# A macaron encoder block on one core: modulation row moved into the gate/up stage, unit loads apart from their splits, an epilogue laid out by a table

## The chip, the cores and the metric

The kernel runs on one core of one Trainium2 chip. The metric is the device time of one execution in microseconds; the time before is the median of three runs. One more execution was taken with the hardware profiler, and all views shown here come from it. In the views PE is TensorE's matmul, PEld its weight load, DVE VectorE, ACT ScalarE, POOL GpSimd, SP the sync engine whose queue issues most DMAs; L200 is line 200 of the kernel. In a list of waits, "A L1 <- B L2: 11.3, 1, 11.3" reads: the instruction A of line 1 stood idle until B of line 2 was done, in total, how often, and the longest.

## What is computed

One layer of an encoder block on x of 1024 tokens by 1024 channels, in float32. A conditioning vector c gives nine rows of 1024 through one large matrix: shift, scale and gate for each of three sub-layers.

```
mod = (silu(c) @ w_ada + b_ada).reshape(b, 3, 3, 1024)
h   = rmsnorm(x, g_pre) * (1 + scale) + shift
x  += res_w * gate * rmsnorm(fn(h), g_post)
fn  = swiglu (FFN 1), mixer (attention and a linear recurrence), swiglu (FFN 2)
swiglu(h) = (silu(h @ w_g) * (h @ w_u)) @ w_down        # 1024 -> 2816 -> 1024
softplus(-lru_lambda)                                     # eight constants per partition of the recurrence
```

## The kernel before

Every float32 product is made of three products of split operands: hi*hi, hi*lo and lo*hi. So every weight that is streamed passes through a split (L142, L143): ScalarE copies the raw tile into hi, then VectorE, or for some units GpSimd, subtracts it for lo. Tiles come from pools with a fixed number of buffers for each tag: `raw` (3), `wh` and `wl` (4 each), `t4` (22 of 4 KB per partition), and in the phase's own pool `u` (3). A DMA waits until the buffer that it is to fill is free. Inside the FFN the order of TensorE, VectorE, ScalarE and GpSimd is the order of the program, and the SP queue's order is the scheduler's, which issues a load as soon as it believes its buffer to be free; the queue itself is in order.

The FFN has two stages, each of which uses a seven-product scheme of block-wise 2x2 multiplication.

The gate/up stage works through 22 blocks of 128 hidden channels, some 19 us each for those in the scheme (blocks 4 to 21 in FFN 1). `block(fb, after)` makes seven products in the order 1, 2, 6, 5, 7, 3, 4, into the PSUM banks psX, psY and psZ. Between them stand evictions: v, a copy of psX by ScalarE (L653), must be made after the vector sum of psY (L640) and a Silu have gone through VectorE and ScalarE, and before product 7 may go on in psX. A tile `pp` with tag u lives from product 5 to product 3. After each product `after(i)` mixes the weights of the next block, advances GpSimd's jobs (sums of pairs for the down stage), and after product 3 advances a generator `early` by one step. That generator loads rows, transposes them into columns, and computes the recurrence's constants: three tiny VectorE instructions, a power on GpSimd (L968), then some twenty-two tiny VectorE instructions (L969 to L984), all in one step.

The down stage streams units of 512 KB (half a pair of activation rows and half a pair of weight rows): eleven units for each of seven passes, in the order 1, 2, 6, 5, 7, 3, 4. A unit takes twelve matmuls. `Units.fetch` loads a unit into a `raw` tile (L839) and splits it at once. `take` keeps three units ahead. In passes 2, 5 and 7 every third split has its lo on GpSimd. Seven of the units of pass 4 (j from KEPT_FROM = 4) are split early, among the units of passes 7 and 3, into t4 tiles, so that pass 4 can end its four accumulators one after the other.

During the down stage of FFN 1 a queue of background generators advances by one step for each unit of the passes 1, 2 and 6: `ada_gate(0)`, which makes the gate row of FFN 1, then `ada_cols(3)` and `ada_cols(4)`, which make the mixer's shift and scale columns. Each loads eight 512 KB blocks of w_ada and adds them up on VectorE with a factor (L198, L200); the row is then spread by matmuls with ones (L289, L290), the columns by eight small matmuls (L214). A generator that needs a PSUM bank yields BANK, and in pass 2 such a step is not taken. After pass 6, `bg_flush` runs what is left.

The epilogue, in and after pass 4, takes each of eight token blocks through `put` (sum of squares on ScalarE L321, its power -1/2 on GpSimd L322 and L323, y times gate L382), `update` (x + r*y on VectorE L388, stored, and its sum of squares) and `norm` (L399). `put` fetches x into `xr`, tag u. In FFN 1 `drain` then transposes the blocks for the next sub-layer and ScalarE evacuates them (L338, L341), while the next phase's first weights are fetched and split. In FFN 2 nothing follows, and `push_last` ends the kernel with two half updates (L443).

Of the kernel before, what the change touches and what calls it, by code (L numbers as in the profile page):

```python
# [10 lines left out]
F32 = mybir.dt.float32  # L11
# [12 lines left out]
P = 128  # L24
# [3 lines left out]
SB = S // P  # L28
# [5 lines left out]
EPS = 1e-6  # L34
NEG = -1e30
HEAD_WAIT = 8
YG_DVE = ()
LATE = 6
FIRST_NEEDS = (1,) * 8
L_WAIT = 11  # L40
# [2 lines left out]
GATES = (2, 0, 2, 4)  # L43
NORM_ACT = ()
DIRECT = {0: 4, 2: 3}
KEPT_FROM = 4


@with_exitstack
def kernel(  # L50
# [7 lines left out]
    nc = tc.nc  # L58
# [18 lines left out]
    def t4(name, dtype=F32, shape=(P, 1024)):  # L77
        return pool.tile(list(shape), dtype, tag="t4", bufs=22, name=nm(name))
# [48 lines left out]
    def load_columns_b():  # L127
        rowsB = tu("rowsB", shape=(P, P))
        nc.scalar.dma_start(rowsB[0:32, :], conv_w.rearrange("o j (k p) -> (o j k) p", p=P))
        for i, v in enumerate((conv_b, lru_ba, lru_bx, lru_lambda)):  # L130
            nc.scalar.dma_start(rowsB[32 + 8 * i : 40 + 8 * i, :], v.rearrange("o (k p) -> (o k) p", p=P))
        yield
        yield
        yield BANK
        pb = trbank("pb")
        nc.tensor.transpose(pb[:, 0:64], rowsB[0:64, :], ident[0:64, 0:64])
        nc.vector.tensor_copy(colsB, pb[:, 0:64])
        yield
# [22 lines left out]
    class Weights:  # L161
# [26 lines left out]
    def ada_acc(v, alloc):  # L188
        acc = alloc("acc")
        for k in range(KB):  # L190
            if raw_home[0] == "t4":
                raw = t4("rawa")
            else:
                raw = wpool.tile([P, 1024], F32, tag="raw", bufs=3, name=nm("rawa"))
            nc.sync.dma_start(raw, w_ada[k * P : (k + 1) * P, v * D : (v + 1) * D])
            yield None
            if k == 0:
                nc.vector.tensor_scalar(acc, raw, c_act[:, 0:1], None, op0=ALU.mult)  # L198
            else:
                nc.vector.scalar_tensor_tensor(  # L200
                    acc, raw, c_act[:, k : k + 1], acc, op0=ALU.mult, op1=ALU.add
                )
        yield None
        yield acc
# [150 lines left out]
    class Epilogue:  # L355
# [4 lines left out]
            self.y, self.r, self.r2, self.xr = {}, {}, {}, {}  # L360
            self.ready = []

        def fetch(self, sb):
            if sb < SB and sb not in self.xr:
                self.xr[sb] = tu("xr")
                nc.sync.dma_start(self.xr[sb], self.xin[sb * P : (sb + 1) * P, :])

        def push(self, sb, y):
# [5 lines left out]
                self.update(sb - 1)  # L374
            self.fetch(sb + 1)

        def put(self, sb, y, eng=None):
            self.fetch(sb)
            self.y[sb] = y
            self.r[sb] = rstd_of(y, self.eps)  # L380
            eng = eng or (nc.vector if sb in YG_DVE or sb == SB - 1 else nc.gpsimd)
            eng.tensor_tensor(y, y, gtile[self.sub], op=ALU.mult)  # L382

        def update(self, sb):
# [85 lines left out]
    def ffn(sub, w_gu, w_down, hh, hl, xin, xout):  # L470
# [217 lines left out]
        def up_phase(started):  # L688

            for fb in range(started, direct):  # L690
                for i in range(2):
                    load(fb, i)
                    cut(fb, i)
            for i in range(2):
                load(direct, i)
            for fb in range(started, direct):
                for k in range(KB):
                    part(fb, 0, k)
                    sum_step()
                finish(fb, 0)  # L700

            def first_needs():
                sum_step(100)
                for i in ORDER[:4]:
                    mix(direct, i)
                    yield
                for kk in range(4):
                    differences(kk)
                    yield
                for i in ORDER[4:]:  # L710
                    mix(direct, i)
# [12 lines left out]
            load(direct + 1, 0)  # L724
            load(direct + 1, 1)
            for fb in range(direct, NF):

                def after(i):
                    mix(fb + 1, i)
                    next(jobs, None)  # L730
                    if i == 3:
                        next(early, None)
                    if fb == NF - 1 and i in ORDER[4:]:
                        units.fetch(ORDER[4:].index(i) + 1)

                ready[0] = fb
                block(fb, after)
                for i in range(2):
                    raws.pop((fb + 1, i), None)
                    load(fb + 2, i)  # L740
            ready[0] = NF
# [80 lines left out]
        class Units:  # L822


            def __init__(self):
                self.order = [(p, j) for p in STREAM for j in range(PAIRS)]

                last, self.order = self.order[-PAIRS:], self.order[:-PAIRS]
                for n, unit in enumerate(last[KEPT_FROM:]):
                    self.order.insert(len(self.order) - 2 * PAIRS + 2 + n * 2, unit)  # L830
                self.order += last[:KEPT_FROM]
                self.n, self.got = 0, {}

            def fetch(self, n):
                while self.n < min(n, len(self.order)):
                    p, j = self.order[self.n]
                    raw = wpool.tile([P, 2, 512], F32, tag="raw", bufs=3, name=nm("rawd"))
                    for o, (t, k, half) in enumerate((act_of[p], down_of[p])):
                        nc.sync.dma_start(raw[:, o], rows(t, 2 * j + k)[:, (h1, h2)[half]])  # L839
                    if p == STREAM[-1] and j >= KEPT_FROM:  # L840
                        hi, lo = t4("dh", F32R, (P, 2, 512)), t4("dl", F32R, (P, 2, 512))
                    else:
                        hi, lo = (wpool.tile([P, 2, 512], F32R, tag=t, bufs=4, name=nm("dh")) for t in ("wh", "wl"))
                    split(raw, hi, lo, nc.gpsimd if p in (2, 5, 7) and j % 3 == 2 else nc.vector)
                    self.got[p, j] = hi, lo
                    self.n += 1

            def take(self, p, j, ahead):
                self.fetch(self.order.index((p, j)) + 1 + ahead)
                return self.got.pop((p, j))  # L850

        units = Units()
# [1 line left out]
        def down_phase(make, ahead):  # L854
# [29 lines left out]
            for p in STREAM[:-1]:  # L884
                own = p in (1, 6, 7)
                dst = chain if own else [bank("pv") for _ in range(4)]
                for j in range(PAIRS):
                    ops = units.take(p, j, 3)
                    for i in range(half):
                        mm(dst[i], i, ops, j == 0 and p not in (6, 7), j == PAIRS - 1)  # L890
                    next(jobs, None)
                    bg(1, own)
                if p == 2:
                    for _ in jobs:
                        pass
                if p == 6:
                    bg_flush()
                    raw_home[0] = "raw"
                for op, sb0, sl in reads[p]:
                    for i in range(half):  # L900
                        op(sb0 + i, sl, dst[i])

            p = STREAM[-1]
            for j in range(KEPT_FROM):
                ops = units.take(p, j, 3)
                for i in range(half):
                    mm(chain[i], i, ops, False, False)
                if j == 0:
                    units.fetch(len(units.order))
                epi.put(j, yacc[j], nc.gpsimd if j % 2 else nc.vector)  # L910
                if j > 0:
                    epi.update(j - 1)
                if j > 1:
                    epi.norm(j - 2)
                if j == KEPT_FROM - 1:
                    epi.update(j)
                    epi.norm(j - 1)
                    epi.norm(j)

            last_steps = {4: ((), (), 0), 5: ((4,), (), 3), 6: ((5,), (4,), 5), 7: ((6,), (5,), KB)}  # L920
            for i in range(half):
# [36 lines left out]
    def lru_constants():  # L958
# [7 lines left out]
        v.tensor_scalar(ax, lam, -1.0, None, op0=ALU.mult)  # L966
        v.tensor_tensor(ax, ax, lam, op=ALU.min)
        nc.gpsimd.tensor_tensor(ee, base, ax, op=ALU.pow)  # L968
        v.tensor_scalar(den, ee, 2.0, None, op0=ALU.add)  # L969
        v.reciprocal(den, den)  # L970
        v.tensor_tensor(s_, ee, den, op=ALU.mult)
# [14 lines left out]

    def mixer_constants():
        yield from load_columns_b()
        lru_constants()
        yield  # L990

    def lru_phase(hh, hl, tail):
# [785 lines left out]
```

## Time and profile before

| | us |
|---|---|
| median of three runs | 2255.58 (2254.29 to 2256.24) |
| the profiled execution | 2258.05, of which the profile's span is 2256.2 |
| TensorE busy in the span | 2163.2 (96%), 9963 matmuls |
| VectorE busy | 1327.2 (59%) |
| ScalarE busy | 1016.5 (45%) |
| GpSimd busy | 786.8 (35%) |

The mean granted clock of TensorE was 0.988 of full speed. FFN 1 fills the span up to about 750 us, FFN 2 the part from about 1590 us to the end. A busy share of TensorE says that matmuls were in flight; whether they ran at the full clock is read from the granted clock beside it. Idle time of the other engines costs nothing unless TensorE waits for it.

### The profile page before, as it was taken

To read this page: it belongs to the slowest core of one execution; us is meant where nothing else is said; L and a number is where in the kernel's file an instruction comes from. 1 tells how busy PE (TensorE), PEld (TensorE's weight loads), DVE (VectorE), ACT (ScalarE), POOL (GpSimd) and SP (SyncE) were. 2 spreads that over 40 slices of the span, in tenths; PEclk is the share of its full clock that TensorE was granted. 3 is DMA by queue.
4 is the path that set the end of the run, shared out by engine and by line. 5 is a ranking of instruction groups with operands and counts; after the bars stand their busy time and mean duration, and the time that the engine had idled before them with its cause. 6 is when DMAs were issued, how large, how long until landed. Compare 5 with 4: busy or idle time off the path is not lost. (4 is left out here: it accounts for less than half of the span.)

```text
span 2256.2 us, 26782 instructions
## 1 busy us (share of the span) xinstructions
PE 2163.2 (96%) x9963; PEld 1789.3 (79%) x9963; DVE 1327.2 (59%) x1680; ACT 1016.5 (45%) x1567; POOL 786.8 (35%) x554
## 2 busy tenths in 40 slices
PE   5999999999799999999999999999999999999998
PEld 3877788887677788888888888888778788888876
DVE  6676665455655677754425665554875665544465
ACT  3543333334244688731137776535443333334443
POOL 3458785421013301100021120005648894522114
PEclk9999999999899999999999999999999999999999
DMA  9337563358666211156511111374247663337665
GB/s 297 105 135 261 205 248 122 121 196 284 230 215 212 86 50 51 58 168 205 195 60 60 43 45 54 101 230 158 94 135 277 235 221 122 114 119 233 197 223 187
DMA packets 269595, 358.37 MB, mean 159 GB/s; under 512 B 16624, under 2 KB 178584, under 8 KB 269464
## 3 DMA queue, kind: packets, MB, share of 16 engines
q1 hardware_dynamic: 256680, 310.48, 42.6%
q10 hardware_dynamic: 12784, 46.18, 5.4%
q8 instruction: 78, 1.28, 0.2%
q14 instruction: 53, 0.43, 0.1%
HBM read 265.37 MB, written 94.37 MB: 159 GB/s over the span
## 5 line engine op out<-in xcount | busy, mean ns | idle before, releaser
L142 ACT CAST dh<-rawd 128x1024 fp32r<-128x1024 f32 x154 | 161.2, 1052 | 229.8 <-DMA rawd<-downs 86.3
L621 DVE TENSOR_TENSOR wm<-raw,wm 128x512 fp32r<-128x512 f32 x152 | 160.1, 1057 | 166.9 <-ACT wm L620 157.3
L143 DVE TENSOR_TENSOR dh<-rawd,dh 128x1024 fp32r<-128x1024 f32 x122 | 158.5, 1303 | 164.9 <-ACT dh L142 159.3
L452 PE MATMUL pj<-hh,wl 128*128 128x512 f32 x576 | 227.8, 396 | 6.3 <-DVE wl L143 4.1
L451 PE MATMUL pj<-hl,wh 128*128 128x512 f32 x576 | 227.4, 395 | 5.5 <-DVE hl L333 5.5
L450 PE MATMUL pj<-hh,wh 128*128 128x512 f32 x576 | 230.1, 400 | 1.6 <-ACT wh L142 1.0
L863 PE MATMUL px<-dh,dh 128*128 128x512 f32 x592 | 184.6, 393 | 5.5 <-POOL dh L143 3.9
L863 PE MATMUL pv<-dh,dh 128*128 128x512 f32 x528 | 166.5, 397 | 1.9 <-DVE dh L143 1.8
L143 POOL TENSOR_TENSOR wl<-raw,wh 128x1024 fp32r<-128x1024 f32 x25 | 61.5, 2469 | 298.6 <-ACT wh L142 254.1
L142 ACT CAST wh<-raw 128x1024 fp32r<-128x1024 f32 (+1 forms) x86 | 86.8, 1010 | 148.2 <-DMA raw<-in_w_in_dram 41.6
L814 POOL TENSOR_TENSOR act<-act,act 128x512 f32<-128x512 f32 x54 | 84.6, 1567 | 157.4 <-DMA act<-act 119.0
L863 PE MATMUL px<-dh 128*128 128x512 f32 x352 | 138.7, 394 | 0.4 <-ACT dh L142 0.4
L322 POOL TENSOR_SCALAR rstd<-rstd 128x1 f32<-128x1 f32 x47 | 33.3, 709 | 300.1 <-ACT junk L321 298.4
L863 PEld LDWEIGHTS px<-dh,dh 128*128 128x128 f32 x592 | 111.2, 189 | 32.0 <-POOL dh L143 4.9
L452 PEld LDWEIGHTS pj<-hh,wl 128*128 128x128 f32 x576 | 109.8, 191 | 31.0 <-DVE wl L143 5.7
L451 PEld LDWEIGHTS pj<-hl,wh 128*128 128x128 f32 x576 | 109.7, 190 | 29.4 <-DVE hl L333 7.4
L143 DVE TENSOR_TENSOR wl<-raw,wh 128x1024 fp32r<-128x1024 f32 (+1 forms) x61 | 77.7, 1274 | 88.9 <-ACT wh L142 88.9
L450 PEld LDWEIGHTS pj<-hh,wh 128*128 128x128 f32 x576 | 109.8, 191 | 24.6 <-ACT wh L142 1.7
L143 POOL TENSOR_TENSOR dh<-rawd,dh 128x1024 fp32r<-128x1024 f32 x18 | 43.0, 2390 | 246.6 <-ACT dh L142 246.6
L630 PE MATMUL psX<-hh,wm 128*128 128x512 f32 x296 | 116.5, 394 | 7.3 <-ACT mixes L653 7.3
L863 PEld LDWEIGHTS pv<-dh,dh 128*128 128x128 f32 x528 | 100.6, 191 | 25.3 <-DVE dh L143 4.3
L630 PE MATMUL psX<-hs,wm 128*128 128x512 f32 x296 | 115.5, 390 | 1.5 <-ACT mixes L646 1.4
(312 smaller groups left out, 5871.9 us busy)
## 6 DMA issues: line engine op xcount, KB each, us to landing
rawa<-in_w_ada_dram SPq DMA_DIRECT2D x56, 512.0 KB, 4.9
raw<-in_ffn_w_gu_dram SPq DMA_DIRECT2D x49, 512.0 KB, 4.6
rawd<-acts SPq DMA_DIRECT2D x88, 256.0 KB, 3.6
rawd<-downs SPq DMA_DIRECT2D x88, 256.0 KB, 3.7
raw<-in_w_in_dram SPq DMA_DIRECT2D x44, 512.0 KB, 3.9
sr<-in_ffn_w_gu_dram SPq DMA_DIRECT2D x39, 512.0 KB, 6.1
act<-act SPq DMA_DIRECT2D x37, 512.0 KB, 5.2
acts<-act ACTq DMA_DIRECT2D x36, 512.0 KB, 3.9
```

The lines of the kernel that those rows point to most:

```text
L142: nc.scalar.copy(hi, raw)
L143: (eng or nc.vector).tensor_tensor(lo, raw, hi.bitcast(F32), op=ALU.subtract)
L322: nc.gpsimd.tensor_scalar(r, r, eps, None, op0=ALU.add)
L450: nc.tensor.matmul(dst, wh[:, kk, :], xhk[:, sl], start=first, stop=False)
L451: nc.tensor.matmul(dst, wh[:, kk, :], xlk[:, sl], start=False, stop=False)
L452: nc.tensor.matmul(dst, wl[:, kk, :], xhk[:, sl], start=False, stop=last)
L621: nc.vector.tensor_tensor(t[:, 1], src, t[:, 0].bitcast(F32), op=ALU.subtract)
L630: nc.tensor.matmul(dst, t[:, 0, kk, :], xh, start=first and kk == 0, stop=False, skip_group_check=True)
L814: nc.gpsimd.tensor_tensor(o, p, q, op=op)
L863: nc.tensor.matmul(dst, a_[:, 0, tk], w_[:, 1, :], start=first and n == 0, stop=last and n == 2, skip_group_check=True,)
```

## The change

Five things are changed.

1. The constants' step has a `yield` behind the GpSimd power, so it takes two blocks. A BANK mark in the generator that loads rows is a plain yield.
2. Once `early` is used up (after block 9 of FFN 1), `after(3)` of each of the blocks 10 to 21 advances the background queue by one step. The raw tiles of w_ada then have the tag u instead of t4.
3. `Units.load` issues a unit's two DMAs, `Units.fetch` does the split. In passes 1, 2 and 6 loads run two units further ahead than splits; every second raw tile of the passes 1, 2, 6 and 5 is a t4 tile. The splits of pass 7 are all on VectorE.
4. KEPT_FROM is 5: five units of pass 4 are streamed and six kept in t4 tiles. The `put`, `update` and `norm` of the first four token blocks stand in the table FIRST_HALF. In both FFNs `put` multiplies by the gate on VectorE for every block; before, it was GpSimd for most.
5. At the start of pass 7 the x rows of the blocks 0 to 3 and 7 are fetched, 3 and 7 into t4 tiles.

```diff
-KEPT_FROM = 4
+KEPT_FROM = 5
+FIRST_HALF = (((0, 1), (), ()), ((2, 3), (0,), ()), ((), (1, 2), ()), ((), (3,), (0, 1)), ((), (), (2, 3)))
...
                 raw = t4("rawa")
+            elif raw_home[0] == "u":
+                raw = tu("rawa")
...
-            eng = eng or (nc.vector if sb in YG_DVE or sb == SB - 1 else nc.gpsimd)
+            eng = nc.vector if self.sub != 1 or sb == SB - 1 else nc.gpsimd
...
                     if i == 3:
-                        next(early, None)
+                        if next(early, BANK) is BANK and sub == 0:
+                            raw_home[0] = "u"
+                            bg(1)
+                            raw_home[0] = "raw"
...
+            def load(self, n):
+                while self.loaded < min(n, len(self.order)):
+                    p, j = self.order[self.loaded]
+                    if self.loaded % 2 and p in STREAM[:4]:
+                        raw = t4("rawd", F32, (P, 2, 512))
+                    else:
+                        raw = wpool.tile([P, 2, 512], F32, tag="raw", bufs=3, name=nm("rawd"))
+                    for o, (t, k, half) in enumerate((act_of[p], down_of[p])):
+                        nc.sync.dma_start(raw[:, o], rows(t, 2 * j + k)[:, (h1, h2)[half]])
+                    self.raws[p, j] = raw
+                    self.loaded += 1
...
-                    split(raw, hi, lo, nc.gpsimd if p in (2, 5, 7) and j % 3 == 2 else nc.vector)
+                    split(raw, hi, lo, nc.gpsimd if p in (2, 5) and j % 3 == 2 else nc.vector)
...
             def take(self, p, j, ahead):
-                self.fetch(self.order.index((p, j)) + 1 + ahead)
+                n = self.order.index((p, j)) + 1
+                self.load(n + ahead + (2 if p in STREAM[:3] else 0))
+                self.fetch(n + ahead)
...
+                if p == 7:
+                    for n in range(half):
+                        epi.fetch(n, tu if n < 3 else t4)
+                    epi.fetch(SB - 1, t4)
...
-                epi.put(j, yacc[j], nc.gpsimd if j % 2 else nc.vector)
-                if j > 0:
-                    epi.update(j - 1)
-                if j > 1:
-                    epi.norm(j - 2)
-                if j == KEPT_FROM - 1:
-                    epi.update(j)
-                    epi.norm(j - 1)
-                    epi.norm(j)
+                puts, updates, norms = FIRST_HALF[j]
+                for n in puts:
+                    epi.put(n, yacc[n])
+                for n in updates:
+                    epi.update(n)
+                for n in norms:
+                    epi.norm(n)
...
         nc.gpsimd.tensor_tensor(ee, base, ax, op=ALU.pow)
+        yield
         v.tensor_scalar(den, ee, 2.0, None, op0=ALU.add)
```

More of the change, by code (lines that the diff above doesn't have):

```diff
@@ L36 @@
 HEAD_WAIT = 8
-YG_DVE = ()
 LATE = 6
@@ L133, in load_columns_b @@
         yield
-        yield BANK
+        yield
         pb = trbank("pb")
@@ L361, in __init__, with fetch @@
             self.ready = []
-        def fetch(self, sb):
+        def fetch(self, sb, alloc=tu):
             if sb < SB and sb not in self.xr:
-                self.xr[sb] = tu("xr")
+                self.xr[sb] = alloc("xr")
                 nc.sync.dma_start(self.xr[sb], self.xin[sb * P : (sb + 1) * P, :])
@@ L375, in push, with put @@
             self.fetch(sb + 1)
-        def put(self, sb, y, eng=None):
+        def put(self, sb, y):
             self.fetch(sb)
@@ L831, in __init__ @@
                 self.order += last[:KEPT_FROM]
-                self.n, self.got = 0, {}
+                self.n, self.loaded, self.got, self.raws = 0, 0, {}, {}
+            def load(self, n):
[9 more added lines that the diff above has]
+                    self.loaded += 1
             def fetch(self, n):
+                self.load(n)
                 while self.n < min(n, len(self.order)):
                     p, j = self.order[self.n]
-                    raw = wpool.tile([P, 2, 512], F32, tag="raw", bufs=3, name=nm("rawd"))
-                    for o, (t, k, half) in enumerate((act_of[p], down_of[p])):
-                        nc.sync.dma_start(raw[:, o], rows(t, 2 * j + k)[:, (h1, h2)[half]])
+                    raw = self.raws.pop((p, j))
                     if p == STREAM[-1] and j >= KEPT_FROM:
@@ L968, in lru_constants @@
         nc.gpsimd.tensor_tensor(ee, base, ax, op=ALU.pow)
+        yield
         v.tensor_scalar(den, ee, 2.0, None, op0=ALU.add)
@@ L988, in mixer_constants @@
         yield from load_columns_b()
-        lru_constants()
+        yield from lru_constants()
         yield
```

## The prediction

> **What bounds the kernel now.** I read the page's busy shares first, then TensorE's waits, then the busy time by stretch, then the order of time in each stretch that loses.
>
> ```profile
> PE 2163.2 (96%) x9963; PEld 1789.3 (79%) x9963; DVE 1327.2 (59%) x1680; ACT 1016.5 (45%) x1567; POOL 786.8 (35%) x554
> PE pc L214 <- DVE acc L200: 11.3, 1, 11.3
> ...
> PE pt L352 <- DVE yacc L399: 4.3, 2, 3.1
> ...
> PE px L863 <- POOL dh L143: 3.9, 2, 1.9
> SPq L366 <- DVE acc L200: 8.0, 1, 8.0
> ```
>
> TensorE is busy for 2163.2 of 2256.2 us and the change takes no matmul away. All that can be won is its idle time, about 93 us, and matmuls that ran at a lower granted clock. The single wait of 11.3 us is the greatest one. The next view gives, by stretch: length, busy time (and count) of PE, PEld, DVE, ACT, POOL, granted clock, DMA share, GB/s.
>
> ```profile
> 240.00:260.00 20.00, 15.41 (x59) 12.26 (x58) 16.42 (x33) 4.87 (x9) 13.70 (x11) 0.83 0.61 215
> 330.00:500.00 170.00, 170.00 (x752) 140.81 (x751) 88.37 (x102) 59.09 (x101) 74.27 (x51) 1.00 0.44 150
> 500.00:532.00 32.00, 28.70 (x115) 22.05 (x114) 27.06 (x21) 14.45 (x18) 7.58 (x5) 0.95 0.68 232
> 532.00:590.00 58.00, 57.12 (x253) 46.90 (x251) 34.95 (x33) 20.61 (x20) 4.79 (x2) 1.00 0.92 321
> 590.00:600.00 10.00, 2.27 (x18) 1.86 (x16) 7.78 (x8) 4.04 (x6) 2.34 (x1) 0.78 0.77 270
> 600.00:610.00 10.00, 6.33 (x23) 5.75 (x24) 5.05 (x6) 0.00 (x0) 0.00 (x0) 0.50 0.20 61
> 610.00:620.00 10.00, 10.00 (x41) 8.13 (x40) 1.97 (x2) 3.16 (x3) 2.40 (x1) 0.87 0.34 109
> 655.00:690.00 35.00, 31.09 (x127) 23.01 (x126) 20.35 (x19) 15.75 (x15) 2.35 (x1) 1.00 0.74 235
> 705.00:770.00 65.00, 56.76 (x250) 45.71 (x249) 40.11 (x37) 38.38 (x62) 42.50 (x39) 0.95 0.49 163
> 2165.00:2195.00 30.00, 27.46 (x110) 21.11 (x109) 17.85 (x16) 13.26 (x14) 2.35 (x1) 0.94 0.73 232
> ```
>
> From 330 to 500 us, in the gate/up stage, TensorE is full (752 matmuls in 170 us, one per 0.226 us), DVE is idle for half the time and DMA for more than half. Everywhere else in the table something is lost, and each of these places belongs to one part of the change.
>
> **The change part by part.**
>
> **(a) The LRU constants.** After the generator's last wait, some 25 tiny DVE instructions run in one burst; the change puts the three before the POOL power and the rest into two blocks of the gate/up stage.
>
> ```profile
> 239.63 1.25 DVE L969 TENSOR_SCALAR sp_den<-sp_ee 128x8 f32<-128x8 f32 x1 [1.77 <-POOL sp_ee L968]
> 248.71 0.16 DVE L984 TENSOR_SCALAR sp_hx<-colsB 128x8 f32<-128x8 f32 x1
> 250.59 0.68 DVE L640 TENSOR_TENSOR mixes<-psY,mixes 128x512 f32<-128x512 f32 x1
> 253.03 0.79 PE L630 MATMUL psX<-hh,wm 128*128 128x512 f32 x1 [4.59 <-ACT mixes L653]
> 253.63 0.63 PE L631 MATMUL psX<-hl,wm 128*128 128x512 f32 x1
> 254.05 0.63 PE L632 MATMUL psX<-hh,wm 128*128 128x512 f32 x1
> ```
>
> The burst holds DVE until 248.8 us, so the eviction of psY comes at 250.59, ScalarE's copy of v after it, and the chain psX waits 4.59 us. The stretch ran at mean clock 0.83, 6.8 us of half rate; 4.6 of them fell on matmuls at 0.42 us apiece instead of 0.226, a loss of 2.2. In all 6.8 us. The change moves only the wait for POOL (1.77 us) and three instructions (about 0.4) out of the burst: 239.63 to 248.8, over 9 us, stays in one piece, a block later. So the wait shrinks by about 2.1 to some 2.5 us, and is not gone. Whether 2.5 us costs the clock is open: the waits of 1.9 us in the stretches at 655 and at 2165 are alike, yet the first kept clock 1.00 and the second fell to 0.94. I take half of a 1.6 us penalty (3.4 us at half rate). Left: 3.3; gain 3.5; ends 0 and 6.8.
>
> [...]
>
> **(b) The first gate row into the gate/up stage.** Twelve steps of ada_gate(0) move from pass 1 of the down stage into after(3) of the blocks 10 to 21: eight 512 KB loads, one product and seven multiply-adds, two splits, four matmuls with ones, and two row loads, which move on SP's queue from about 475-511 to about 320-480 us. Their DVE prices:
>
> ```profile
> L200 DVE SCALAR_TENSOR_TENSOR acc<-rawa,c_act,acc x49: 1270/1284/1287, 506.4 to 1089.2; 128x1024 f32<-128x1024 f32 x49
> PE pg L289 <- ACT acch L142: 1.4, 1, 1.4
> PE pg L289 <- DVE yacc L876: 0.9, 1, 0.9
> PE pg L290 <- DVE acch L143: 0.6, 1, 0.6
> PE px L863 <- DVE dh L143: 1.2, 2, 0.7
> ```
>
> One 1.28 us instruction per 19 us block: from 330 to 500 us DVE has 82 us free. If that cover were gone, the 15 us of DVE would show whole; but even the 11 us burst of (a) cost 4.6. The load sits in a u tile; three exist, one holds the sum, one the block's pp, so each load waits for pp or for the last raw row and lands a block ahead of its use. The ones-matmuls come a whole block after their split, so PE does not wait for them. New cost taken: 0; ends -3 (a gain has no cause) and 0. In the down stage their three waits (2.9) go, and the half-rate clock at 500 to 532 (0.05 of 32 us, 3.2 us at half, 1.5 lost). Column work (ada_cols) then fills pass 1 with the same DVE load, so the two dh waits there (1.2) go only in part, by the earlier raw loads: 0.6. Gain 5.0; ends 3 and 5.9.
>
> **(c) The flush.** Before, ada_gate(0) and two ada_cols, 12+11+11 steps, had 33 units, but a step that needs a bank is not taken in pass 2, so it halted there; the flush after pass 6 then ran eight products one after another (the 11.3 us), with SP blocked for 8.0 us behind the same tile. After, the ada_cols need 11 + 11 steps: eleven in pass 1, ten in pass 2, the last in the first unit of pass 6. The flush finds nothing. Its clock goes too: 0.22 of the ten us to 600, 0.50 of the next, 0.13 of the third make 17 us of half rate, of which 9 (603.7 to 612.6) fell on matmuls, a loss of 9 x (1 - 0.226/0.42) = 4.2. Gain 15.5; ends 13 and 15.5. What is late next: pass 2 takes eight multiply-adds (10 us) that it did not have; 532 to 590 already ran both kinds of work with only 0.9 us idle, at DMA share 0.92, and 16 rows instead of 24 now load around it.
>
> **(d) Epilogue of the first FFN.** All y times gate go to DVE, xr is fetched at pass 7, and the norms follow a table with five streamed units in front.
>
> ```profile
> L382 POOL TENSOR_TENSOR yacc<-yacc,gate x10: 2354/2395/3248, 714.7 to 2245.1; 128x1024 f32<-128x1024 f32 x10
> L382 DVE TENSOR_TENSOR yacc<-yacc,gate x5: 1215/1227/3422, 711.1 to 2224.0; 128x1024 f32<-128x1024 f32 x5
> L388 DVE SCALAR_TENSOR_TENSOR xr<-yacc,rstd,xr x15: 1272/1284/2991, 712.7 to 2247.5; 128x1024 f32<-128x1024 f32 x15
> L321 ACT ACTIVATE junk<-yacc x15: 1041/1057/1059, 708.9 to 2241.8; 128x1024 bf16<-128x1024 f32 x15
> 747.18 0.77 ACT L338 ACTIVATE hh<-pt,scol,acol 128x512 fp32r<-128x512 f32 x1
> 753.83 0.63 ACT L873 COPY yacc<-px 128x512 f32<-128x512 f32 x1
> 760.87 2.35 POOL L143 TENSOR_TENSOR wl<-raw,wh 128x1024 fp32r<-128x1024 f32 x1
> ```
>
> The stretch loses 8.2 us idle and 3.1 us of clock (0.05 of 65 us, 6.5 us at half). DVE needs about 19 us from 706 for four sums, one split, four products (1.23), four updates (1.28) and four norms (0.75), so the norms are done near 725, before the transposes at 728: those 4.3 us of wait go. But ScalarE is late next. It evacuates eight transposed blocks at 1.33 us each (five take 747.18 to 753.83), and before each group stand copy 0.6, square 1.25, DVE product 1.23, DVE update 1.28, square 1.25, weight cast 1.0: 6.6 us in a chain. Counted from the end of block 5 at 728.1: first three evictions at 734.8, the five others at 745.4 (before 747.18), copy 752.0, square, product, update, square and cast to 758.1, POOL's split of the weight to 760.6 (before 763.2). TensorE waits for that split, so 2.6 us come through. Ends -2 and 9.
>
> **(e), (f) Streamed units in passes 7 and 3 of both FFNs.** They lose 3.9 us at 655 to 690, and 2.5 plus 1.7 of clock at 2165 to 2195, in waits for dh. The deeper loads act in passes 1, 2 and 6 only; here it is three splits that go from POOL (about 2.4 us) to DVE (1.23) and one unit less to stream (28 instead of 29). I leave a quarter of it: gains 3.0 and 3.5; ends 0 and 8.1 together. Of the t4 tiles, 8 yacc + 12 kept halves + 2 xr make 22, all there are, as 8 + 14 did before.
>
> **(g) The tail.**
>
> ```profile
> 2245.53 0.39 PE L863 MATMUL px<-dh,dl 128*128 128x512 f32 x1
> 2247.53 1.28 DVE L388 SCALAR_TENSOR_TENSOR xr<-yacc,rstd,xr 128x1024 f32<-128x1024 f32 x1 [2.79 <-POOL yacc L382]
> 2249.34 0.15 DVE L440 SCALAR_TENSOR_TENSOR rstd<-sq,sq 128x1 f32<-128x1 f32 x1
> 2249.56 0.55 POOL L441 TENSOR_TENSOR rstd<-rstd,nhalf 128x1 f32<-128x1 f32 x1 [2.07 <-DVE rstd L440]
> 2251.40 1.42 DVE L443 SCALAR_TENSOR_TENSOR xr<-yacc,rstd,xr 128x512 f32<-128x512 f32 x2 [1.91 <-DMA xr<-x]
> ```
>
> The last matmul ends at 2245.9; the last update starts at 2251.40, first behind POOL's product of block 6, then behind the load of xr. The product on DVE ends near 2244.2, the update of block 6 near 2246.5, the half product (0.6) near 2247.1, sum and power near 2248.0, and xr has been there since pass 7: 2248.1. Gain 3.3; ends 1.2 (only the load) and 3.8.
>
> **Sum.** 3.5 + 5.0 + 15.5 + 2.6 + 3.0 + 3.5 + 3.3 = 36.4. The profiled execution took 2258.05 (span 2256.2), so its like would take 2221.6; from the median of 2255.58 that is **2219 us**. A measurement of this kernel can tell about 0.2%, 4.5 us, from no change.
>
> **The rivals.**
>
> **All waits go.** With (a) 6.8, (b) 5.9, (c) 15.5, (d) 9, (e, f) 8.1 and (g) 3.8 the gain is 49: 2206. For it: each has its own cure. Against: the 9 us burst and ScalarE's chain are still there.
>
> **Only what is taken off the path bodily pays.** DVE, with three splits, ten products of 1.23 us and all its old work, becomes the last to finish in the epilogue, and three raw buffers still pace passes 7 and 3: (d), (e) and (f) give 0. Then 27: 2228. For it: DVE is busy 20 of 35 us at 655 and 40 of 65 at 705. Against: POOL's 2.4 us instructions, now gone, stood in those very waits.
>
> **The burst grows.** Five of its tiny instructions took 1.0 to 1.25 us instead of 0.17 (the first and the last row of (a) are one of each), each ending as a POOL instruction of 1.3 us ended. If POOL ran through all of the 20 in their new block, 15 more would wait about 1 us: (a) turns from +3.5 to about -11, and the time is 2234. Against: in the old block POOL had work for five only. [...]
>
> **Slower.** The SP queue is in order: a gate row waiting for a u tile holds the weights of the next blocks behind it, in blocks 10 to 21, as the 8.0 us of SP show it can. If every block lost what the burst cost (4.6 and 2.2 of clock), that is 82 us: 2301. It decides from 3.0 us per block. Against: weights are loaded more than a block ahead, and pp is read out just ahead of the step.
>
> **How the numbers follow.** Forecast 0.48, all waits go 0.15, only the bodily parts 0.26, burst grows 0.06, slower 0.05. Bounds of the small terms around the forecast alone give 2211 to 2226; taking in the second and third case, and the fourth but for its top, the range is 2206 to 2232. Faster by over 0.2%: 0.94 (all cases but the last, less a little); within 0.02; slower 0.04.
>
> **What would show it.** (a) A wait psX on mixes of about 2.5 us one block later. (b) Rows of w_ada in the gate/up stage from about 320 us, still 170 us full. (c) No wait pc on acc over 1 us, clock 1.00 from 590 to 620. (d) No wait pt on yacc, but pj still waiting for wl. (e, f) No wait px on POOL dh in pass 7. (g) The last update within 2.5 us of the last matmul. Wrong would make it: gaps in every block from 320 to 490 us, SP waiting at L195, or DVE full from 700 to 770.

## The result, and the profile after

The changed kernel takes **2230.77 us** (median of four runs, 2227.76 to 2234.47) where the kernel before takes 2255.91 (2254.29 to 2257.37): a ratio of 0.9889, interval 0.9872 to 0.9907. That is 25.1 us less, or 26.6 by the spans of the two profiled executions. The forecast was 2219 us with a gain of 36.4. The direction and the range held, but between a quarter and a third of the gain is missing.

One correction first. The description of the change says that the x rows are fetched at the start of pass 7, and steps (d) and (g) count on pass 7. In the code `if p == 7:` stands behind the loop over the units, so these fetches come at the **end** of pass 7. In FFN 1 the three into u tiles are issued ahead of that (572 to 577 us), the two into t4 tiles at 645.77 us, as pass 7 ends. Most of the error in the forecast comes from these two loads, as the experiments show; what they would cost at the start of pass 7 was not tried.

The first view after is the page's busy line and the list of TensorE's waits (in total, how often, the longest).

```profile
PE 2156.7 (97%) x9963; PEld 1785.0 (80%) x9963; DVE 1332.4 (60%) x1696; ACT 1016.1 (46%) x1567; POOL 758.2 (34%) x538
PE psX L633 <- ACT mixes L656: 4.3, 3, 2.3
...
PE pv L882 <- ACT dh L143: 4.1, 3, 2.2
...
PE pt L355 <- ACT h L344: 2.8, 3, 1.1
PE psZ L633 <- ACT pp L660: 2.4, 2, 1.8
...
PE pj L455 <- POOL wl L144: 2.2, 1, 2.2
PE pj L453 <- ACT h L344: 1.9, 1, 1.9
```

Three great waits of before are gone: pc on acc (11.3), pt on yacc (4.3), px on POOL dh (3.9). What is late next is ScalarE, in `pv <- ACT dh` and `pj <- ACT h`. The same stretches as in the prediction, by time, show where TensorE is now full (length, busy time and count of PE, PEld, DVE, ACT, POOL, granted clock, DMA share, GB/s):

```profile
257.00:277.00 20.00, 16.89 (x72) 13.03 (x71) 15.08 (x34) 4.87 (x9) 11.97 (x10) 1.00 0.71 235
330.00:491.00 161.00, 160.36 (x705) 132.00 (x705) 91.40 (x108) 56.85 (x98) 72.90 (x50) 1.00 0.48 158
491.00:523.00 32.00, 32.00 (x151) 26.79 (x150) 28.75 (x24) 14.84 (x17) 11.08 (x5) 1.00 0.94 324
523.00:584.00 61.00, 61.00 (x278) 50.73 (x277) 38.57 (x33) 23.12 (x24) 5.67 (x3) 1.00 0.88 308
584.00:614.00 30.00, 30.00 (x134) 24.84 (x133) 11.77 (x11) 13.82 (x16) 6.34 (x3) 1.00 0.33 111
614.00:645.00 31.00, 30.07 (x131) 24.18 (x130) 18.45 (x17) 15.58 (x16) 0.00 (x0) 1.00 0.71 225
645.00:680.00 35.00, 32.00 (x137) 25.37 (x136) 18.97 (x19) 14.70 (x14) 0.00 (x0) 1.00 0.71 239
680.00:742.00 62.00, 55.75 (x245) 44.83 (x245) 41.72 (x42) 39.04 (x63) 31.99 (x34) 0.94 0.46 154
2123.00:2154.00 31.00, 30.27 (x134) 24.52 (x133) 18.87 (x18) 15.91 (x17) 0.00 (x0) 1.00 0.71 231
2154.00:2191.00 37.00, 32.79 (x134) 25.87 (x133) 19.39 (x19) 14.70 (x14) 0.00 (x0) 0.95 0.72 232
```

From 491 to 614 us, the down stage's passes 1, 2, 6 and 5, TensorE is full at full clock; before, the stretch from 590 to 610 alone held 8.6 us of work in 20. The gate/up stage from 330 to 491 us, which now also carries the gate row, stays full too. What is lost stands in the first row (257) and most of all in the last rows: passes 3 of both FFNs (645 and 2154 us) and the epilogue (680).

A table by stage, worked out from TensorE's rows as the time from the first matmul of one stage or pass to the first of the next (a pass of 132 matmuls that nothing holds up takes 29.9, as pass 5 does after):

| us | before | after | forecast gain | gain |
|---|---|---|---|---|
| gate/up stage of FFN 1: (a) | 354.5 | 353.3 | 3.5 | 1.2 |
| FFN 1 passes 1, 2, 6, 5: (b), (c) | 147.8 | 123.4 | 20.5 | 24.4 |
| FFN 1 passes 7, 3: (e) | 66.6 | 65.7 | 3.0 | 1.0 |
| FFN 1 pass 4 and on to the next stage: (d) | 88.6 | 86.5 | 2.6 | 2.1 |
| FFN 2 passes 7, 3: (f) | 65.4 | 68.0 | 3.5 | -2.6 |
| from the last matmul's start to the end: (g) | 10.7 | 8.2 | 3.3 | 2.5 |
| the rest (mixer, gate/up of FFN 2, other passes) | | | 0 | -2.0 |

Four matmuls with ones (0.9 us) moved from the second row into the first, so the rest of that stage gave about 2.1. The last row is mostly in the gate/up stage of FFN 2 (364.9 before, 366.6 after, with a granted clock of 0.93 from 1735 to 1760 us); a second execution of the same changed kernel took 364.7 there, so it belongs to no step.

### The profile page after: what moved, and what is told of

Read it like the earlier page. It is cut to its first block, busy times and chain, and to the rows that moved or that the text cites. A ratio compares the mean times of both kernels' runs of the same rounds, so it can differ in the third digit from the quotient of the medians.

```text
span 2229.6 us, 26752 instructions
## 1 busy us (share of the span) xinstructions
PE 2156.7 (97%) x9963; PEld 1785.0 (80%) x9963; DVE 1332.4 (60%) x1696; ACT 1016.1 (46%) x1567; POOL 758.2 (34%) x538
## 3 DMA queue, kind: packets, MB, share of 16 engines
q8 instruction: 78, 1.28, 0.2%
## 5 line engine op out<-in xcount | busy, mean ns | idle before, releaser
L454 PEld LDWEIGHTS pj<-hl,wh 128*128 128x128 f32 x576 | 110.0, 191 | 29.9 <-DVE hl L336 7.6
L623 ACT CAST wm<-raw 128x512 fp32r<-128x512 f32 x152 | 92.6, 613 | 52.1 <-POOL raw L611 52.0
```

The lines of the kernel that those rows point to most:

```text
L454: nc.tensor.matmul(dst, wh[:, kk, :], xlk[:, sl], start=False, stop=False)
L623: nc.scalar.copy(t[:, 0], src)
```

## The experiments

Each ratio is to runs of the kernel before on the same chip. All were timed in five rounds.

**The three parts of the change alone.** rows_only is the kernel before with items 1 and 2 (the constants' step cut in two, w_ada rows in the blocks 10 to 21). stream_only is the kernel before with item 3, epi_only with items 4 and 5.

```diff
 rows_only (on the kernel before)
+            elif raw_home[0] == "u":
+                raw = tu("rawa")
...
-                        next(early, None)
+                        if next(early, BANK) is BANK and sub == 0:
+                            raw_home[0] = "u"
+                            bg(1)
+                            raw_home[0] = "raw"
...
+        yield
...
 stream_only (on the kernel before)
+            def load(self, n):
...
-                    split(raw, hi, lo, nc.gpsimd if p in (2, 5, 7) and j % 3 == 2 else nc.vector)
+                    split(raw, hi, lo, nc.gpsimd if p in (2, 5) and j % 3 == 2 else nc.vector)
...
 epi_only (on the kernel before)
-KEPT_FROM = 4
+KEPT_FROM = 5
+FIRST_HALF = (((0, 1), (), ()), ((2, 3), (0,), ()), ((), (1, 2), ()), ((), (3,), (0, 1)), ((), (), (2, 3)))
...
+                if p == 7:
+                    for n in range(half):
+                        epi.fetch(n, tu if n < 3 else t4)
+                    epi.fetch(SB - 1, t4)
```

> The kernel before with the first two things of the change alone: the wait step behind the POOL power and the first gate row in blocks 10 to 21. The theory that the flush carries the change: the passes 1 to 5 gain some 22 to 24 us, the gate/up stage 0 to 3, and passes 7 and 3 and the epilogue and tail stay as they were: 2255.9 - 23 = 2233, so at least as good as nine tenths of the whole change. The rival, that deeper raw loads are needed for the gain in passes 1 to 6 (the dh waits of 1.2 us and small gaps): 2238 or more.

> The kernel before with the third thing alone: loads issued apart from splits, every second raw tile of four passes in t4, pass 7 split on VectorE alone; seven kept units as before. If raw loads ahead and the GpSimd splits were what kept passes 1 and 7 waiting, pass 1 loses its two dh waits (1.2 us) and passes 7 and 3 lose 2 us less in FFN 1 and 3 us less (with the clock) in FFN 2: 2250. The flush of 11.3 us stays. If the three raw tiles of passes 7 and 3 are the limit and the engine of the split is not, nothing moves: 2254 to 2257.

> The kernel before with the fourth and fifth thing alone: five streamed units of pass 4, the table, the products with the gate on VectorE, the x rows fetched at the end of pass 7. Theory 1 (x loads in the stream): epilogue +2.4 and tail +2.5 us are won, but passes 7 and 3 lose 2 to 5 us more in each FFN, with 7.5 us for the half unit behind the x loads: 2253 to 2258, about no change. Rival (x loads cost nothing): 2251, the gains of epilogue and tail.

| | median us | ratio | interval |
|---|---|---|---|
| rows_only | 2238.22 | 0.9928 | 0.9915 to 0.9942 |
| stream_only | 2245.68 | 0.9955 | 0.9943 to 0.9968 |
| epi_only | 2257.34 | 1.0009 | 1.0000 to 1.0017 |

By the ratios, of 2255 us, that is -16.2, -10.1 and +2.0: together -24.3, against -25 for the whole. By the medians the parts add up, and two thirds of the gain is the row that moved. Stage by stage they overlap: in the profiled executions rows_only wins 20.5 us in passes 1, 2, 6 and 5 of FFN 1, stream_only 9.3, and the whole change 24.4, for both take away waits of passes 1 and 6, those of the matmuls with ones among them. So the close agreement of the sums, with intervals of some 2 to 3 us each, is in part luck. The median of rows_only misses the 2233 of its theory and lands on the 2238 of the rival, by which the deeper loads are needed too; its runs lie from 2233.53 to 2242.21, and the profiled one is the fastest. stream_only wins 10 us where 5 were expected. One row of rows_only's stretches, then the wait that stream_only and epi_only keep, in that order:

```profile
580.00:614.00 34.00, 34.00 (x151) 28.15 (x150) 11.27 (x10) 16.00 (x18) 7.21 (x3) 1.00 0.62 191
```

```profile
PE pc L214 <- DVE acc L200: 10.2, 1, 10.2
```

```profile
PE pc L216 <- DVE acc L202: 10.4, 1, 10.4
```

So the flush goes with the moved row and with nothing else. In the table's terms rows_only takes pass 6 from 48.5 to 32.2 and pass 5 from 32.6 to 29.9. stream_only takes pass 1 from 35.1 to 30.4, pass 6 from 48.5 to 45.9 and pass 7, where it moves the splits to VectorE, from 33.8 to 31.3.

epi_only came out as its first theory had it: the epilogue's part alone wins nothing. Its pass 4 takes 37.0 instead of 40.7 and its tail 8.2 instead of 10.7, yet FFN 2's passes 7 and 3 take 35.9 and 32.7 instead of 34.5 and 30.9. Its x loads go out as pass 7 ends (2181.96 us), so they can account for pass 3 alone; the 1.4 us of pass 7 stay open. What such loads do in pass 3 is seen in the changed kernel's chain of work that ended last (start, us, what):

```profile
2147.41 4.59 DMA rawd<-in_ffn_w_down_dram
...
2155.27 0.43 SPq L369
2155.75 7.58 DMA rawd<-in_ffn_w_down_dram
2163.43 1.05 ACT dh L143
2165.78 26.14 PE pv L882 x107
```

The SP queue's own order at that place, and ScalarE's casts behind it, with their idle time in brackets:

```profile
2154.44 0.32 SPq L848 DMA_DIRECT2D rawd<-acts  x1
2154.80 0.91 SPq L369 DMA_DIRECT2D xr<-x  x2
2155.75 0.43 SPq L848 DMA_DIRECT2D rawd<-in_ffn_w_down_dram  x1
...
2163.43 1.04 ACT L143 CAST dh<-rawd 128x1024 fp32r<-128x1024 f32 x1 [5.24 <-DMA rawd<-in_ffn_w_down_dram]
```

L369 is the load of x. Two loads of 512 KB stand ahead of half a unit of 256 KB, which then takes 7.58 us to land where its neighbour took 4.59. ScalarE waits 5.24 us for it, and TensorE after ScalarE. In FFN 1 the same two loads are issued at 645.77 us. This suggests: the loads cost what the splits won.

**The x loads one pass earlier in the program.**

```diff
-                if p == 7:
+                if p == 6:
```

> The changed kernel with one thing moved: the x rows for the epilogue are fetched at the end of pass 6 instead of at the end of pass 7. Theory 1 (two x loads stand between the two halves of a streamed unit): in the FFN 2 of the changed kernel the two xr loads are issued at 2154.8, and the half unit issued behind them takes 7.58 us where its neighbours take 3 to 4.6; TensorE then loses 5.1 us in pass 3 (4.7 in FFN 1) and 1.6 us of clock. With the loads out of that stretch passes 7 and 3 of each FFN should lose under 2.5 us each, and the time should fall by 5 to 8 us, to about 2224. Theory 2 (three raw tiles simply cannot feed 28 units in two passes): the same loss of 4 to 6 us comes in each FFN wherever the x rows are fetched, the half unit takes 3 to 5 us but its successors are late all the same, and the time stays within 2 us of 2231.

2223.25 us, ratio 0.9857 (0.9844 to 0.9871). In FFN 1 the x loads now go out between 565 and 574 us, in pass 6; in FFN 2 the two go out at 2053.0 and 2055.2 us, near the end of pass 2 already, since the queue's issue runs ahead of the program. The passes in which they now run take no longer for it: passes 1, 2, 6 and 5 together take 123.4 us in FFN 1 and 119.7 in FFN 2, as in the changed kernel. The stretches of passes 7 and 3 read:

```profile
614.00:645.00 31.00, 30.80 (x135) 24.89 (x134) 18.19 (x16) 16.00 (x16) 0.00 (x0) 1.00 0.72 232
645.00:677.00 32.00, 30.36 (x132) 24.28 (x131) 19.86 (x19) 13.69 (x14) 0.00 (x0) 1.00 0.71 229
...
2153.00:2184.00 31.00, 30.19 (x132) 24.31 (x131) 18.86 (x19) 14.17 (x14) 0.00 (x0) 1.00 0.69 227
```

Passes 7 and 3 together take 63.1 and 63.0, against 65.7 and 68.0 in the changed kernel. The difference sits in pass 3, behind the place of the loads: 34.1 and 36.9 us in the changed kernel (35.3 and 34.6 in a second execution), 32.4 and 31.4 here, while pass 7 moves by less than 1 us. But 3.3 and 3.2 us are still lost, where the theory of the loads expected under 2.5: a part of the second theory, the three raw tiles, stays. By the spread of runs alone the changed kernel, run again (below), differs from this by only 4 us with intervals that overlap; it is the passes that carry the reading.

**Queue or traffic?** The same two loads, at the same place, on ScalarE's queue. The first run of it left the time open (its runs lay from 2222 to 2230), so it was run again beside the changed kernel.

```diff
-                nc.sync.dma_start(self.xr[sb], self.xin[sb * P : (sb + 1) * P, :])
+                (nc.scalar if alloc is t4 else nc.sync).dma_start(self.xr[sb], self.xin[sb * P : (sb + 1) * P, :])
```

> The changed kernel with the two t4 x loads (blocks 3 and 7) issued on ScalarE's queue instead of SP's, at the same place at the end of pass 7. If it was the place in the SP queue that hurt (0.9 us of issue between the two halves of a unit), passes 7 and 3 lose only 1 us less than in the changed kernel; if 1 MB of DMA at about 240 GB/s is the cost (4.4 us for the unit behind it), the half unit beside them still takes 6 to 8 us and the loss stays; either way 2229 to 2231. If on the ScalarE queue the two loads fall earlier, when the stretch has slack, as with xr_pass6: 2224.

> The changed kernel unaltered, as the measure for the three beside it. 2228 to 2233.

> xr_actq once more, beside the changed kernel: its trace kept the loss in passes 7 and 3 (68.2 and 65.6 us for the two passes, against 65.7 and 68.0 in the changed kernel and 63.1 in both FFNs of xr_pass6), but its median lay near xr_pass6. If the 1 MB of DMA is the cost and not the place in the SP queue, the two times agree within 2 us; if the place counts, xr_actq is 5 us or more faster.

| | median us | ratio | interval | passes 7 + 3, FFN 1 and FFN 2 |
|---|---|---|---|---|
| xr_actq | 2223.85 | 0.9862 | 0.9843 to 0.9880 | 68.3, 65.6 |
| after_again | 2227.29 | 0.9873 | 0.9860 to 0.9886 | 66.3, 65.7 |
| xr_actq_again | 2228.31 | 0.9878 | 0.9865 to 0.9892 | 66.4, 65.4 |

The two kernels are alike. The load's place in SP's queue is not what costs; the megabyte that moves at that moment is. xr_actq's DMA issues from 640 to 665 us (count, KB each, median us to landing) show what it does to the units beside it:

```profile
rawd<-acts SPq DMA_DIRECT2D x9, 256.0 KB, 4.6
rawd<-in_ffn_w_down_dram SPq DMA_DIRECT2D x8, 256.0 KB, 4.8
xr<-in_x_dram ACTq DMA_DIRECT2D x2, 512.0 KB, 8.5
```

Without the x loads there, in xr_pass6 from 645 to 660 us, the same two kinds take 3.6 and 3.9 (and the same again from 640 to 665):

```profile
rawd<-acts SPq DMA_DIRECT2D x6, 256.0 KB, 3.6
rawd<-in_ffn_w_down_dram SPq DMA_DIRECT2D x6, 256.0 KB, 3.9
```

**The splits of pass 7 back on GpSimd.** This weighs the step that (e) and (f) were priced by, with the x loads out of the way.

```diff
 (on xr_pass6)
-                    split(raw, hi, lo, nc.gpsimd if p in (2, 5) and j % 3 == 2 else nc.vector)
+                    split(raw, hi, lo, nc.gpsimd if p in (2, 5, 7) and j % 3 == 2 else nc.vector)
```

> xr_pass6 with the three splits of pass 7 back on GpSimd (2.4 us each instead of 1.23 on VectorE). If the engine of these splits sets the pace of passes 7 and 3 (prediction steps e and f), pass 7 waits for GpSimd's dh again, 2 us in each FFN, with half clock perhaps 1.6 more: 2226 to 2230. If the three raw tiles and the DMAs set it, no change: 2223.

2228.11 us, ratio 0.9879 (0.9863 to 0.9895), 4.9 us more than xr_pass6. TensorE's waits from 640 to 700 us begin with:

```profile
PE px L882 <- POOL dh L144: 1.9, 1, 1.9
```

That is the wait of before, back again. The passes 7 and 3 take 66.4 and 67.7 where xr_pass6 takes 63.1 and 63.0: 3.3 and 4.6, against the 3.0 and 3.5 of the forecast. The mechanism of (e) and (f) was right and its size nearly so; the loads beside it were not counted.

**Two smaller terms.** evac_share gives half of the second group's evictions of transposed blocks to VectorE. burst3 cuts the burst of the constants once more, by a yield in its loop, and drops another yield of the generator so that the number of its steps stays.

```diff
 evac_share (on xr_pass6)
-                    epi.drain(n_out, on_act=(1, 1))
+                    epi.drain(n_out, on_act=(1, 0))
 burst3 (on xr_pass6)
-        yield
...
+            if q == 9:
+                yield
```

> xr_pass6 (x rows fetched at the end of pass 6) with one more edit: in the epilogue of FFN 1 the second of every two transposed blocks has its float32 copy made by VectorE instead of ScalarE (on_act (1, 0) instead of (1, 1)). If ScalarE's chain of evictions is what comes late after the transposes (prediction step d), eight evictions get 0.67 us shorter every other time, 2.7 us in all, and the wait pj for h (3.6 us in xr_pass6, with a half clock of 6.8 us that cost up to 3) shrinks by 2 to 5: 2219 to 2221. If VectorE, which has all the products with the gate now, is as full as ScalarE, nothing moves or it gets worse: 2223 or more.

> xr_pass6 with one more edit: the recurrence's constants in three steps instead of two (one idle step ahead of them is dropped, so that the gate row still begins in block 10). If the rest of the burst (257.7 to 264.0 us in the changed kernel) makes the two waits of 1.3 and 2.0 us at 268 and 272 us, both go: 3.3 us less, 2220. If only the first wait (psX) is the burst's and the second (psZ) comes from GpSimd, which waits for a DMA from 262.7 to 267.5 us, 1.3 us go and 2.0 stay: 2222.

2222.32 us, 0.9848 (0.9833 to 0.9864), and 2222.58 us, 0.9848 (0.9830 to 0.9865): each within 1 us of xr_pass6 (2 us by the ratios), so as times both are inconclusive. At their own places they did something: evac_share shortens the part behind pass 4 from 49.5 to 47.4, and burst3 the wait of psX. TensorE's waits from 235 to 290 us, xr_pass6 first, then burst3:

```profile
PE psZ L633 <- ACT pp L660: 1.9, 1, 1.9
PE psX L633 <- ACT mixes L656: 1.1, 1, 1.1
```

```profile
PE psZ L632 <- ACT pp L659: 2.1, 1, 2.1
PE psX L632 <- ACT mixes L655: 0.6, 1, 0.6
```

The burst sets psX's wait; the second wait does not care about it, as the second case of its expectation had it. In the changed kernel GpSimd waits 4.9 us there for a load of its own job, which may be behind it; that wasn't tested.

**All of it, and one buffer kind more.** combo is xr_pass6, burst3 and evac_share together. combo_raw7 also lets every second raw tile of pass 7 be a t4 tile, and loads of pass 5 run two units further ahead.

```diff
 (combo_raw7 on combo)
-                    if self.loaded % 2 and p in STREAM[:4]:
+                    if self.loaded % 2 and p in STREAM[:5]:
...
-                self.load(n + ahead + (2 if p in STREAM[:3] else 0))
+                self.load(n + ahead + (2 if p in STREAM[:4] else 0))
```

> xr_pass6 with burst3 and evac_share together. By the places of the two traces 0.9 us (gate/up) and 2.1 us (after pass 4) are won and do not touch: 2219 to 2221, if the two small gains are real; 2223 if they are noise or are given back.

> combo, with every second raw tile of pass 7 in t4 too, and loads two units further ahead in pass 5 as well. If the three raw tiles still pace passes 7 and 3 (3.3 us lost in each FFN in xr_pass6), the loss falls below 1.5 us in each FFN: 3 to 4 us faster than combo, 2216 to 2218. If the splits or the DMA engines set it, no change.

combo takes 2219.40 us, 0.9841 (0.9827 to 0.9854), as expected if the two small gains are real; combo_raw7 takes **2212.14 us, 0.9806 (0.9793 to 0.9820)**. It beats both kernels: 44 us under the kernel before as it ran beside it, and some 15 to 19 under the changed one in its two sets of runs. Against combo it wins 7.3 us by the medians and 5.2 by the profiled executions, more than the 3 to 4 expected; passes 7 and 3 give 2.4 and 3.0 of it (62.2 and 62.8 in combo, 59.8 in both FFNs here). Their rows in combo_raw7:

```profile
614.00:644.00 30.00, 30.00 (x134) 24.85 (x133) 21.12 (x20) 17.58 (x18) 0.00 (x0) 1.00 0.76 252
644.00:674.00 30.00, 30.00 (x134) 24.85 (x133) 16.81 (x17) 12.12 (x13) 0.00 (x0) 1.00 0.64 212
2113.00:2143.00 30.00, 30.00 (x134) 24.86 (x133) 20.34 (x19) 17.84 (x19) 0.00 (x0) 1.00 0.72 232
2143.00:2173.00 30.00, 30.00 (x134) 24.86 (x133) 17.70 (x17) 12.62 (x13) 0.00 (x0) 1.00 0.72 235
```

TensorE is full in all four, at a DMA rate (212 to 252 GB/s) like that of the kernels that lose there (225 to 239 in the changed kernel). So it was not bandwidth over the stretch, but loads that did not run far enough ahead. Whether the further tiles or the greater depth in pass 5 cured it was not separated.

## Why the prediction was right or wrong

**(a)** Half right. The waits of the changed kernel from 262 to 275 us:

```profile
POOL act L820 <- DMA act<-act: 4.9, 1, 4.9
...
PE psZ L633 <- ACT pp L660: 1.8, 1, 1.8
PE psX L633 <- ACT mixes L656: 1.2, 1, 1.2
```

The wait psX on mixes is still there one block later, as forecast, but at 1.2 us instead of 2.5, because the burst met GpSimd less: it took 6.3 us (257.70 to 264.03), and only two of its tiny instructions took 1.15 us or so instead of 0.17, each ending as one of the two GpSimd instructions of 1.3 us there ended (261.30 and 262.68). A second wait, psZ on pp (1.8 us), came in its block and was not forecast. The clock stayed at 1.00 (row 257 to 277), and the half chance given to a penalty was not needed. The two waits, 3.0 us, come close to the 3.3 that the forecast left, but that is luck: the one wait is half of what was forecast, and the other was not in it. Over the whole stage 2.1 us were won instead of 3.5, with what the gate row costs there (below) already taken off.

**(b), (c)** Right, and under-sized: 24.4 (or 23.5 without the four matmuls) instead of 20.5. There was no flush to run, as counted, and block by block the gate/up stage took up the row's twelve steps at a cost of 0.6 us in 161. What was missed is the deeper loads: rows_only, without them, still waits for dh in pass 1 and runs at a granted clock of 0.5 from 525.0 to 528.4 us, and takes 127.3 us for the four passes where the changed kernel takes 123.4. That is 3.9 us, where the forecast gave them 0.6 for the wait on dh. This surplus hides a part of what is missing elsewhere.

**(d)** Right. Norms came early enough, pt on yacc is gone, and ScalarE's chain is late next: pass 4 wins 3.7 us, and behind it 1.6 are given back, in `pj <- ACT h` (1.9) and `pj <- POOL wl` (2.2). 2.1 against 2.6. Which of the two is late varies: a second execution has 3.5 and 0.3. epi_only shows the same 3.7 and 1.6, and evac_share the 2.1 us that ScalarE's evictions hold.

**(e), (f)** This is where the forecast failed. Its terms for the splits were sound (though a quarter left of the 2.5 + 1.7 us of (f) gives 3.2, not 3.5): xr_pass6 wins 3.5 and 2.3 against the kernel before in the two FFNs, together nearly 6 of the 6.5 forecast. The step that failed is that the x loads were put at nothing: (d) and (g) count only that they come early enough, in (g)'s words that "xr has been there since pass 7". They are issued as pass 7 ends, a megabyte into a stretch that the same text said three raw buffers pace. In the two executions of the changed kernel passes 7 and 3 of both FFNs took 133.6 and 132.0 against 132.0 before, so the whole of 6.5 was used up. The rival that gave (d), (e) and (f) nothing, at 2228, came nearer to the measured time than the forecast, and its "three raw buffers still pace passes 7 and 3" fits combo_raw7, which takes away all that is lost there. Its other half, VectorE as the last to finish in the epilogue, does not hold in FFN 1: evac_share gives VectorE more work there, and the part behind pass 4 gets 2.1 us shorter.

**(g)** 2.5 of 3.3. VectorE's order in the tail, then GpSimd's powers:

```profile
2219.61 1.23 DVE L385 TENSOR_TENSOR yacc<-yacc,gate 128x1024 f32<-128x1024 f32 x1 [1.66 <-ACT junk L324]
2220.75 1.28 DVE L391 SCALAR_TENSOR_TENSOR xr<-yacc,rstd,xr 128x1024 f32<-128x1024 f32 x1
...
2222.55 1.28 DVE L391 SCALAR_TENSOR_TENSOR xr<-yacc,rstd,xr 128x1024 f32<-128x1024 f32 x1
...
2225.15 1.41 DVE L446 SCALAR_TENSOR_TENSOR xr<-yacc,rstd,xr 128x512 f32<-128x512 f32 x2 [0.66 <-POOL rstd L444]
...
2220.99 1.46 POOL L326 TENSOR_TENSOR rstd<-rstd,nhalf 128x1 f32<-128x1 f32 x1
2224.57 0.55 POOL L444 TENSOR_TENSOR rstd<-rstd,nhalf 128x1 f32<-128x1 f32 x1 [2.12 <-DVE rstd L443]
```

The last matmul ends near 2221.85, so the last update follows it by 3.3 us: before it was 5.5, forecast 2.2, and the sign of "within 2.5 us" did not come. The load of xr is no longer in the chain and GpSimd's product neither, as forecast. What the sum had too early is the update of block 6 (2222.55), and two things end just ahead of it. On VectorE the update of the block before (2220.75, 1.28 us) now stands between the product and it. GpSimd's power for block 6 ends only at 2222.45, 0.6 us behind the last matmul, where the kernel before had it 0.75 us ahead. The power's own chain starts later, since a block has six kept units instead of seven (ScalarE's copy of block 6 starts 4.05 us ahead of the last matmul's end, before 4.72), and it takes 1.46 us beside VectorE's update, where the next one, with VectorE idle, takes 0.55. No run separates the two.

The slower rival did not come up. From 330 to 614 us the list of TensorE's waits has one line, so a queue held up behind the u tiles reached nothing:

```profile
PE psZ L633 <- ACT pp L660: 0.6, 1, 0.6
```

## What to carry to other kernels

Find the place of a prefetch in the order of issue, in the code and in the trace, before it is put at nothing: it is not only whether it comes early enough, but what it runs beside. Here the stretch that is fed through three buffers had no room for other transfers (pass 3 took 34.1 and 36.9 us with them, 32.4 and 31.4 without), though the DMA's share was 0.71 to 0.72; such loads belong where a stretch has slack (issued in pass 6 of FFN 1 and near the end of pass 2 of FFN 2 they left 123.4 and 119.7 us for four passes as they were), and buffers and depth added to passes 7 and 5 (5 to 7 us) were worth more than any shift of work between the engines that was tried. Background work that is spread over slots pays when it fits them to the last step, so that nothing is left to be flushed (rows_only, 20.5 us in four passes).

## What the runs showed of the hardware

Behind two loads of 512 KB a 256 KB load took 7.58 us where its neighbour took 4.59 (6.67 and 4.61 in a second execution), and for the kernel's time it made no difference whether they came from the same queue or from another (2227.29 and 2228.31 us).

Behind short waits the granted clock fell or did not. In the changed kernel it stayed at 1.00 with waits of 1.2 and 1.8 us near 270 us, and behind one of 2.2 and one of 0.8 us just before 2166 us the row reads 0.95. Two executions of this kernel traded places in the same passes: the first had 1.00 in FFN 1's pass 3 and 0.95 in FFN 2's, the second, of which the rows follow, the reverse. In FFN 1's pass 3 the waits of the two are alike: the longest is 1.4 us in both, the next 0.8.

```profile
645.00:680.00 35.00, 32.11 (x133) 25.56 (x132) 19.80 (x19) 14.44 (x14) 0.00 (x0) 0.95 0.72 240
...
2151.00:2186.00 35.00, 31.44 (x135) 24.90 (x135) 18.87 (x19) 14.67 (x14) 0.00 (x0) 1.00 0.74 235
```

The waits behind which the clock fell in pass 3 were each of 2.2 us or less. Where it fell, as from 2166.0 to 2169.4 us, a matmul took 0.43 us instead of 0.227, which costs some 3.4 us x 0.47 = 1.6 us. In the kernel before, the half rate behind a wait of 1.9 us lasted 3.4 us too (2175.9 to 2179.3), the length that the forecast's 1.6 us counts with. So after a wait of about 2 us that price stands as a chance, not as a certainty; these runs do not show how long a wait must be for it.
